# Layer 1's attention begun nine slots earlier, with short logits sharing a bank, biases loaded a group ahead, and GpSimd scaling by a column operand

## The chip, the cores and the metric

The kernel runs on one core of a Trainium2 chip. The metric is the time of one execution on the device, in microseconds (us). A core has a matrix engine (PE), three engines for elementwise work (DVE, the vector engine; ACT, the scalar engine; POOL, the GpSimd engine) and DMA queues, here driven by SP. Each engine takes its own instructions in order, and engines wait for each other through semaphores. PE writes into PSUM, which has eight banks of 512 float32 columns on 128 partitions; POOL cannot reach PSUM.

## The reference

Two layers on a sequence of 512 tokens of width 1024. Layer 0 mixes a stick-breaking attention with a short convolution, layer 1 is a sparse attention, and each is followed by a SwiGLU network. The change lies in layer 1's attention:

```python
def odd_mixer(h, w_in, q_gain, k_gain, w_out, rel_bias):
    proj = h @ w_in
    q, k, v, qi, ki, wi = jnp.split(proj, offsets([ATT_WIDTH, KV_WIDTH, KV_WIDTH, ...]), axis=-1)
    q = rms_norm(q.reshape(b, s, ATT_HEADS, HEAD_DIM), q_gain)     # 16 heads of 64
    k = rms_norm(k.reshape(b, s, KV_HEADS, HEAD_DIM), k_gain)      # 4 groups, 4 heads each
    ...
# dsa_attention, for each block of 128 queries:
        score = ...                                # indexer; the best 128 keys of each query are kept
        logits = (jnp.einsum('bqgrd,bqkgd->bqgrk', qb, k_sel) * HEAD_DIM ** -0.5 + bias)
        p = jax.nn.softmax(logits, axis=-1)
        return jnp.einsum('bqgrk,bqkgd->bqgrd', p, v_sel)
```

Instead of gathering keys, the kernel adds a mask of -1e30 to the logits of keys that were not chosen. Matrix operands are kept as a high and a low half (fp32r), so that a product is made of two or three matmuls.

## The kernel before

**Slots and events.** The projections are loops over weight tiles. After each three matmuls of 128x512 (`mm3`, or lines 232 to 234) they call `slot()`, which counts on and runs what `after(n, fn, key)` has put down for this slot, smaller keys first. So attention is woven into projections: its instructions stand, on every engine, at the places where the slots put them. In layer 1 this written order is kept for PE, DVE, ACT and POOL (`L1_ORDER`). When a projection is over, empty slots follow, in which nothing but attention stands.

**The projections of layer 1** come in this order: indexer, keys and values, queries of heads 0 to 7 (`ev_q0`), queries of heads 8 to 15 (`ev_q1`, the last query projection, 32 slots), then, after the empty slots, the output projection in two halves. At the end of the last query projection ACT copies each of its four results (`qn<-acc`) and squares it (`sq`, `sqx<-acc`, L966), DVE sums the squares (L967), and `head_norm` makes a reciprocal root of them on ACT (`hn_y`, L979), some small steps on DVE, and four products on POOL (L987). `turn_q` then transposes the queries (L999, tile `pt`) and `stack` writes their high half on ACT (L494) and the low half on POOL or DVE (L498); POOL works from a copy in SBUF (`qt`, L1045).

**Top-k.** DVE finds the kept keys by 16 rounds of MAX (L934) and MATCH_REPLACE (L937) on three query blocks, spread over the projections, and then writes the masks (L940). Query block 0 needs none.

**Attention** has 16 units, numbered n: group g = n // 4 (four heads) and query block qb = n % 4. A unit of query block qb has (qb + 1) x 128 keys, so logits are 128, 256, 384 or 512 wide. Unit n goes through these steps, at slots counted from its first, b:

- `logits` (b to b + 3, one head per slot): two matmuls (L507, L508) into one of two `z` banks, a third that adds the mask (L1084, not for qb = 0), and one DVE instruction that adds the bias and finds the maximum (L1085). For qb = 0 it also issues the DMA of the head's bias table, with four buffers (`rb`).
- `exps` (b + 4 to b + 7): DVE negates the four maxima (L1093); ACT makes exp and sum, one head per slot (L1095).
- `norms` (b + 8, b + 9): DVE takes the reciprocals `sm` (L1102); heads 0, 1 and 3 are scaled on POOL (L1105), head 2 on DVE (L1110).
- `turn_p` (b + 11 and on, one block of keys per slot): four transposes (L1118, tile `pt`), a high half on ACT (L1129), a low half on DVE (L1130).
- `prod` (b + 14 and on): six matmuls per block of keys into `po` (lines 105 to 107); then `keep` on ACT (L1150) and DVE (L1151).

Unit n begins at slot b = 4n + 32 - EARLY of the last query projection, with EARLY = 2.

Of the kernel before, what the change touches and what calls it, by code (L numbers as in the profile page):

```python
# [8 lines left out]
F32 = mybir.dt.float32  # L9
F32R = mybir.dt.float32r  # L10
ALU = mybir.AluOpType
# [4 lines left out]
P = 128  # L16
S = 512
# [14 lines left out]
LAG_K, T1P, B2, LAG_KLO, P1 = 2, 3, 'adbc', 2, 0  # L32
EARLY, SQ_ACT = 3, 256
DOT_PACE = 1
# [6 lines left out]
FILL = -3e38  # L41
# [1 line left out]
ARENA_KB = 104.5  # L43
X_SPANS = ((0, 1), (1, 2), (2, 4), (4, 6), (6, 8))

EARLY = 2
T1P = 4
LAG_K = 3
NORM_POOL = (0, 1, 3)
# [27 lines left out]
class Net:  # L77
# [762 lines left out]
    def layer1_mix(self):  # L840
        nc, I, tc = self.nc, self.I, self.tc
# [10 lines left out]
        qs, qsf = self.R(72.5, 16, S)  # L852
# [3 lines left out]
        with ExitStack() as es:  # L856
            sp = es.enter_context(tc.tile_pool(name="l1", bufs=2))
# [3 lines left out]
                    for qb in range(TB)]  # L861
            score = [None] + [wide[qb]()[:, 0] for qb in (1, 2)] + [self.ssq]
            mask = [None] + [sp.tile([P, (qb + 1) * P], F32R, name=f"mask{qb}", bufs=1)
                             for qb in (1, 2, 3)]
            eye = self.eye
# [77 lines left out]
            for qb, pace in zip((1, 2, 3), PACE):  # L943
                for r in range(16):
                    t = dots[qb] - self.slots + int(pace * r)
# [25 lines left out]
            def head_norm(hn, raw, dst, nh, pace):  # L971

                a, y, t = hn["a"], hn["y"], hn["t"]

                def chain():
                    nc.vector.tensor_tensor(a, a, r2.unsqueeze(2).to_broadcast([P, TB, nh]),
                                            op=ALU.mult)
                    nc.vector.tensor_scalar(a, a, EPS, None, op0=ALU.add)
                    nc.scalar.activation(y, a, AF.Abs_reciprocal_sqrt)  # L979

                def chain2():
                    self.newton(y, a, t)
                    nc.vector.tensor_tensor(y, y, self.rcol.unsqueeze(2).to_broadcast([P, TB, nh]),
                                            op=ALU.mult)

                def norm(tb):
                    nc.gpsimd.tensor_tensor(dst[tb], raw[tb],  # L987
                                            y[:, tb].unsqueeze(2).to_broadcast([P, nh, 64]),
                                            op=ALU.mult)
                self.after(2, chain, -1)  # L990
                self.after(LAG_CH, chain2, -1)
                for tb in range(TB):
                    self.after(LAG_CH + 1 + int(pace * tb), lambda tb=tb: norm(tb), 7)
                return LAG_CH + 1 + int(pace * 4)

            def turn(src, c, tag):
                pt = self.bank(tag, "pt")
                for tb in range(TB):
                    nc.tensor.transpose(pt[:, tb * P:(tb + 1) * P], src[tb][:, c * P:(c + 1) * P],  # L999
                                        self.ident)  # L1000
                return pt
# [17 lines left out]
            t = head_norm(hk, [t[:, :, 1] for t in d], [t[:, :, 0] for t in d], 4, 1)  # L1019
# [20 lines left out]
            def turn_q(qn, hf, c, tag):  # L1040
                pt = turn(qn, c, tag)

                if c in Q_POOL[hf]:
                    src, eng = self.wraw.tile([P, S], F32, name="qt", tag="raw"), nc.gpsimd
                    nc.scalar.copy(src, pt)  # L1045
                else:
                    src, eng = pt, nc.vector
                self.stack([(qs[:, h], qsf[:, h]) for h in (8 * hf + 2 * c, 8 * hf + 2 * c + 1)],
                            src, eng, LAG_LO)
# [10 lines left out]
            t = head_norm(h0, heads(q0[0]), heads(q0[0]), 8, 1.7)  # L1060
# [3 lines left out]
            order = [(qb, g) for g in range(4) for qb in range(TB)]  # L1064
            bias, us = {}, [{} for _ in order]

            def logits(n, r):
                (qb, g), u = order[n], us[n]
                nk = (qb + 1) * P
                t = slice(qb * P, nk)  # L1070
                h = 4 * g + r
                if r == 0:
                    u["mx"] = sp.tile([P, TB], F32, name="mx", bufs=3)
                    u["sm"] = sp.tile([P, TB], F32, name="sm", bufs=3)
                    u["ls"] = wide[qb]()
                if not qb:
                    bias[h] = sp.tile([P, S], F32, name="bias", tag="rb", bufs=4)
                    nc.sync.dma_start(bias[h], bass.AP(tensor=self.F.tensor,
                                                       offset=self.F.offset + h * 640,
                                                       ap=[[1, P], [1, S]]))  # L1080
                z = self.bank("z", "z")[:, 0:nk]
                self.qk(z, qs[:, h, t], kh[:, g, 0:nk], kl[:, g, 0:nk], not qb)
                if qb:
                    nc.tensor.matmul(z, eye, mask[qb], start=False, stop=True)  # L1084
                nc.vector.tensor_tensor_reduce(out=u["ls"][:, r], in0=z,  # L1085
                                               in1=bias[h][:, 0:nk][:, ::-1],
                                               scale=1.0, scalar=FILL, op0=ALU.add,
                                               op1=ALU.max, accum_out=u["mx"][:, r:r + 1])

            def exps(n, rs):  # L1090
                ls, mx, sm = us[n]["ls"], us[n]["mx"], us[n]["sm"]
                if rs[0] == 0:
                    nc.vector.tensor_scalar(mx, mx, -1.0, None, op0=ALU.mult)  # L1093
                for r in rs:
                    nc.scalar.activation(ls[:, r], ls[:, r], AF.Exp, bias=mx[:, r:r + 1],  # L1095
                                         accum_out=sm[:, r:r + 1])

            def norms(n, rs):
                ls, sm = us[n]["ls"], us[n]["sm"]
                nk = (order[n][0] + 1) * P  # L1100
                if rs[0] == 0:
                    nc.vector.reciprocal(sm, sm)  # L1102
                for r in rs:
                    if r in NORM_POOL:
                        nc.gpsimd.tensor_tensor(ls[:, r], ls[:, r],  # L1105
                                                sm[:, r:r + 1].to_broadcast([P, nk]), op=ALU.mult)
                    elif r in NORM_ACT:
                        nc.scalar.activation(ls[:, r], ls[:, r], AF.Copy, scale=sm[:, r:r + 1])
                    else:
                        nc.vector.tensor_scalar(ls[:, r], ls[:, r], sm[:, r:r + 1], None,  # L1110
                                                op0=ALU.mult)

            def turn_p(n, kb):
                u = us[n]
                self.turns += 1
                pt = self.bank("tbd"[self.turns % 3], "pt")
                for r in range(4):
                    nc.tensor.transpose(pt[:, r * P:(r + 1) * P],  # L1118
                                        u["ls"][:, r, kb * P:(kb + 1) * P], self.ident)
                i = self.turns % 4  # L1120
                if n >= 8 and i >= 2:

                    ph, pl = (sp.tile([P, S], F32R, name="pT", tag=f"n{2 * i - 4 + j}", bufs=1)
                              for j in range(2))
                    phf = ph.bitcast(F32)
                else:
                    o = (48.25, 52.25, 8, 12)[i]
                    (ph, phf), pl = self.R(o, S), self.R(o + 2, S)[0]
                nc.scalar.copy(ph, pt)  # L1129
                self.after(LAG_LO, lambda: nc.vector.tensor_tensor(pl, pt, phf, op=ALU.subtract), -1)  # L1130
                u[kb] = [p.rearrange("p (c e q) -> p c e q", c=2, e=2) for p in (ph, pl)]
# [13 lines left out]
            def keep(n):  # L1145
# [5 lines left out]
                self.after(LAG_K, lambda: nc.vector.tensor_tensor(  # L1151
                    al[:, c, t], po, ahf[:, c, t], op=ALU.subtract), -2)

            for n, (qb, g) in enumerate(order):
                b = 4 * n + 32 - EARLY
                for r in range(4):
                    self.after(b + r, lambda n=n, r=r: logits(n, r), 0)
                for r in range(4):
                    self.after(b + 4 + r // EXPS, lambda n=n, r=r: exps(n, (r,)), 0.5)
                    self.after(b + LAG_N + r // 2, lambda n=n, r=r: norms(n, (r,)), 3)  # L1160
                for kb in range(qb + 1):
                    self.after(b + LAG_C + kb, lambda n=n, kb=kb: turn_p(n, kb), 1)
                    self.after(b + LAG_C + LAG_P + kb, lambda n=n, kb=kb: prod(n, kb), 2)
                self.after(b + LAG_C + LAG_P + qb + 1, lambda n=n: keep(n), -1)
            start = self.slots + 32 - EARLY

# [10 lines left out]
            t = head_norm(h1, heads(q1), heads(q1), 8, 1)  # L1177
# [62 lines left out]
```

## Time and profile before

| | |
|---|---|
| median of 3 runs | 1212.41 us (1212.17 to 1212.91) |
| the profiled execution | 1214.13 us, of which its span 1212.4 us |
| PE busy | 1189.0 us, 98% of the span |
| PEld (weight loads) busy | 978.5 us |
| DVE, ACT, POOL busy | 652.9, 480.1, 143.8 us |
| the last query projection's end | about 700.3 us |
| attention without a projection | about 700 to 764 us |

Busy time is what the records of an engine cover. A matmul of 128x512 is recorded as 0.39 us, but the next one begins 0.23 us later, so PE counts as busy through short waits. Rows of the timeline give start, length, engine, line, operation, the tiles written and read, and in brackets how long the engine stood idle before and what ended it. An `x3` at the end merges neighbours into one row. `LDWEIGHTS` rows are left out here.

### The profile page before, as it was taken

The numbers are of one execution on the slowest core, as the hardware profiler recorded it, in microseconds if no ns is written. First come the engines' busy times: TensorE is split into PE (matmuls) and PEld (weight loads), VectorE is DVE, ScalarE is ACT, GpSimd is POOL, SyncE is SP. The second block draws the span as 40 slices with busy tenths as digits, with TensorE's granted clock in tenths as the row PEclk, the third lists the DMA queues.
The fourth block names the chain that finished last, engine by engine and source line by source line (L and its number), as shares of the span: only waits on it lengthen the run. The fifth ranks groups of instructions, "written<-read, shape, count | busy, mean of one in ns | idle before, by whom it ended". The sixth has DMA issues, their size and how long they took to land.

```text
span 1212.4 us, 14654 instructions
## 1 busy us (share of the span) xinstructions
PE 1189.0 (98%) x5547; PEld 978.5 (81%) x5547; DVE 652.9 (54%) x1067; ACT 480.1 (40%) x797; POOL 143.8 (12%) x217
## 2 busy tenths in 40 slices
PE   9999999999999999999999989999999999999998
PEld 7777878888888888888788868888888888888886
DVE  5679965655545443333379977745444343342222
ACT  5556634543434332222253577534332322322120
POOL 1234300200000000011001554312000000000000
PEclk9999999999999999999999999999999999999999
DMA  5322125878887632232346432223333333332430
GB/s 191 92 70 70 53 84 190 277 248 281 284 273 262 226 92 96 96 96 78 124 150 232 157 104 70 71 78 126 91 89 90 103 87 102 89 104 88 129 97 35
DMA packets 118583, 159.86 MB, mean 132 GB/s; under 512 B 6292, under 2 KB 91840, under 8 KB 118512
## 3 DMA queue, kind: packets, MB, share of 16 engines
q1 hardware_dynamic: 117712, 157.73, 40.1%
q10 hardware_dynamic: 800, 1.18, 0.3%
q8 instruction: 44, 0.72, 0.2%
q14 instruction: 27, 0.22, 0.1%
HBM read 131.00 MB, written 27.89 MB: 131 GB/s over the span
## 4 chain that ended last, share of the span: by engine, by line
PE 89%; DVE 6%; issue 2%; POOL 2%; ACT 0%; DMA 0%; POOLq 0%; DVEq 0%; ACTq 0%
PE acc L105 22%; PE acc L107 21%; PE acc L106 21%; PE acc L234 6%; PE acc L233 6%; PE acc L232 6%; PE pt L1118 1%; PE z L507 1%; PE z L508 1%; DVE om L532 1%; DVE wl L163 1%; PE po L106 1%; PE po L107 1%; DVE be L535 1%; PE po L105 1%
## 5 line engine op out<-in xcount | busy, mean ns | idle before, releaser
L105 PE MATMUL acc<-arena,wh 128*128 128x512 f32 (+2 forms) x1176 | 466.7, 397 | 1.9 <-DVE xT L728 1.0
L107 PE MATMUL acc<-arena,wl 128*128 128x512 f32 (+2 forms) x1176 | 458.2, 390 | 0.1
L106 PE MATMUL acc<-arena,wh 128*128 128x512 f32 (+2 forms) x1176 | 458.0, 389 | 0.0
L163 DVE TENSOR_TENSOR wl<-raw,wh 128x1024 fp32r<-128x1024 f32 (+1 forms) x167 | 202.9, 1215 | 285.3 <-ACT wh L162 285.0
L162 ACT CAST wh<-raw 128x1024 fp32r<-128x1024 f32 (+1 forms) x167 | 173.0, 1036 | 360.5 <-PE acc L106 155.7
L107 PEld LDWEIGHTS acc<-arena,wl 128*128 128x128 f32 (+1 forms) x1176 | 220.4, 187 | 49.9 <-DVE wl L163 0.4
L105 PEld LDWEIGHTS acc<-arena,wh 128*128 128x128 f32 (+1 forms) x1176 | 220.8, 188 | 46.9 <-DVE xT L728 2.1
L106 PEld LDWEIGHTS acc<-arena,wh 128*128 128x128 f32 (+1 forms) x1176 | 220.8, 188 | 43.6 <-issue 0.7
L232 PE MATMUL acc<-wh,arena 128*128 128x512 f32 x272 | 108.8, 400 | 0.0
L234 PE MATMUL acc<-wh,arena 128*128 128x512 f32 x272 | 108.4, 399 | 0.0
L233 PE MATMUL acc<-wl,arena 128*128 128x512 f32 x272 | 108.2, 398 | 0.0
L286 POOL TENSOR_TENSOR ssq<-ssq,sqx 128x512 f32<-128x512 f32 x12 | 18.2, 1520 | 371.7 <-ACT sqx L285 371.7
L234 PEld LDWEIGHTS acc<-wh,arena 128*128 128x128 f32 x272 | 51.5, 189 | 12.2
L815 DVE TENSOR_TENSOR pwl<-praw,pwh 128x1024 fp32r<-128x1024 f32 (+1 forms) x25 | 30.2, 1208 | 57.0 <-ACT pwh L814 57.0
L233 PEld LDWEIGHTS acc<-wl,arena 128*128 128x128 f32 x272 | 51.5, 189 | 11.6
L232 PEld LDWEIGHTS acc<-wh,arena 128*128 128x128 f32 x272 | 51.5, 189 | 11.5
L763 DVE TENSOR_TENSOR ft<-acc,rbc 128x512 f32<-128x512 f32 x44 | 30.0, 690 | 45.7 <-PE acc L107 45.6
L814 ACT CAST pwh<-praw 128x1024 fp32r<-128x1024 f32 (+1 forms) x25 | 25.9, 1036 | 68.5 <-DMA praw<-in_od_w_in_dram 38.2
L765 ACT ACTIVATE fs<-ft 128x512 f32<-128x512 f32 x44 | 27.6, 629 | 51.3 <-DVE ft L763 51.3
L507 PE MATMUL z<-arena 128*128 128x384 f32 (+3 forms) x120 | 40.7, 342 | 6.7 <-DVE mx L1085 4.1
L1085 DVE CUSTOM_DVE_ANT_0 L<-z,bias 128x128 f32<-128x128 f32 (+3 forms) x64 | 30.7, 485 | 22.2 <-PE z L1084 19.6
L770 DVE TENSOR_TENSOR fp<-acc,fs 128x512 f32<-128x512 f32 x44 | 30.4, 690 | 22.7 <-PE acc L107 22.7
(212 smaller groups left out, 1281.0 us busy)
## 6 DMA issues: line engine op xcount, KB each, us to landing
raw<-in_ffn_w_gate_dram SPq DMA_DIRECT2D x44, 512.0 KB, 3.7
raw<-in_ffn_w_up_dram SPq DMA_DIRECT2D x44, 512.0 KB, 3.8
raw<-in_ffn_w_down_dram SPq DMA_DIRECT2D x42, 512.0 KB, 3.7
l1h<-pwh SPq DMA_DIRECT2D x24, 512.0 KB, 2.7
l1l<-pwl SPq DMA_DIRECT2D x24, 512.0 KB, 3.1
wh<-l1h SPq DMA_DIRECT2D x24, 512.0 KB, 4.0
wl<-l1l SPq DMA_DIRECT2D x24, 512.0 KB, 4.5
raw<-in_ev_w_in_dram SPq DMA_DIRECT2D x23, 512.0 KB, 3.9
```

The lines of the kernel that those rows point to most:

```text
L105: mm(ps, wh, xh, start=first, stop=False)
L106: mm(ps, wh, xl, start=False, stop=False)
L107: mm(ps, wl, xh, start=False, stop=last)
L162: nc.scalar.copy(wh, raw)
L163: (lo or nc.vector).tensor_tensor(wl, raw, wh.bitcast(F32), op=ALU.subtract)
L232: mm(ps[tb], h[:, t], wh[:, k], start=c == 0, stop=False)
L233: mm(ps[tb], h[:, t], wl[:, k], start=False, stop=False)
L234: mm(ps[tb], l[:, t], wh[:, k], start=False, stop=c == kc - 1)
L507: self.nc.tensor.matmul(z, qs, kd, start=True, stop=False)
L770: nc.vector.tensor_tensor(p, ps, sil[m], op=ALU.mult)
L815: nc.vector.tensor_tensor(l, raw, h.bitcast(F32), op=ALU.subtract)
L1085: nc.vector.tensor_tensor_reduce(out=u["ls"][:, r], in0=z, in1=bias[h][:, 0:nk][:, ::-1], scale=1.0, scalar=FILL, op0=ALU.add, op1=ALU.max ...
```

## The change

It does six things, all in layer 1's attention (lines of the changed code are some 10 to 16 higher than before: L1085 becomes L1097, L1095 becomes L1107, L1105 becomes L1117, L1118 becomes L1130, L1173 becomes L1189).

1. EARLY goes from 2 to 11: unit n begins nine slots earlier in the program. Unit 0 now begins at slot 21 of 32 of the last query projection, and its first `turn_p` follows on that projection's last slot. The empty slots before the output projection become nine fewer. What the query projection's own events do (`turn_q`) stays at its slots.
2. Logits of query block 0 are made four heads in a slot into one `z` bank, of block 1 two heads per slot and bank; blocks 2 and 3 stay at one.
3. Biases are loaded by `load_bias`, 14 slots ahead of their group: two heads into one buffer of the pool that otherwise holds raw weights (`raw`, three buffers), two into `rb`.
4. The copies `qt` of the last queries use another buffer (`tmp`, one of it) instead of `raw`.
5. The count that picks banks and buffers in `turn_p` starts anew.
6. POOL scales by `tensor_scalar` with a column of 128x1 as the operand, instead of `tensor_tensor` with that column broadcast.

```diff
-EARLY = 2
+EARLY = 11
...
-                    src, eng = self.wraw.tile([P, S], F32, name="qt", tag="raw"), nc.gpsimd
+                    src = (sp.tile([P, S], F32, name="qt", tag="tmp", bufs=1) if hf else
+                           self.wraw.tile([P, S], F32, name="qt", tag="raw"))
+                    eng = nc.gpsimd
...
+            def load_bias(g):
+                pair = self.wraw.tile([P, 2, S], F32, name="bias2", tag="raw")
+                for r in range(4):
+                    h = 4 * g + r
+                    bias[h] = (pair[:, r] if r < 2 else
+                               sp.tile([P, S], F32, name="bias", tag="rb", bufs=4))
+                    nc.sync.dma_start(bias[h], ...)
...
-            def logits(n, r):
+            def logits(n, rs):
...
-                z = self.bank("z", "z")[:, 0:nk]
-                self.qk(z, qs[:, h, t], kh[:, g, 0:nk], kl[:, g, 0:nk], not qb)
...
+                bank = self.bank("z", "z")
+                zs = [bank[:, i * nk:(i + 1) * nk] for i in range(len(rs))]
+                for r, z in zip(rs, zs):
+                    h = 4 * g + r
+                    self.qk(z, qs[:, h, t], kh[:, g, 0:nk], kl[:, g, 0:nk], not qb)
+                    if qb:
+                        nc.tensor.matmul(z, eye, mask[qb], start=False, stop=True)
+                for r, z in zip(rs, zs):
+                    nc.vector.tensor_tensor_reduce(...)
...
-                        nc.gpsimd.tensor_tensor(ls[:, r], ls[:, r],
-                                                sm[:, r:r + 1].to_broadcast([P, nk]), op=ALU.mult)
+                        nc.gpsimd.tensor_scalar(ls[:, r], ls[:, r], sm[:, r:r + 1], None,
+                                                op0=ALU.mult)
...
+            self.turns = -1
+            for g in range(4):
+                self.after(max(1, 16 * g + 32 - EARLY - 14), lambda g=g: load_bias(g), -3)
             for n, (qb, g) in enumerate(order):
                 b = 4 * n + 32 - EARLY
-                for r in range(4):
-                    self.after(b + r, lambda n=n, r=r: logits(n, r), 0)
+                w = (4, 2, 1, 1)[qb]
+                for r in range(0, 4, w):
+                    self.after(b + r, lambda n=n, rs=tuple(range(r, r + w)): logits(n, rs), 0)
```

**PE, in the last query projection, just after the third transposition of the first queries.** L232 to L234 are one slot of the projection. Before:

```order
L999 MATMUL pt<-eye,qn 128x128 x4
L232 MATMUL acc<-wh,arena 128x512
L233 MATMUL acc<-wl,arena 128x512
L234 MATMUL acc<-wh,arena 128x512
L232 MATMUL acc<-wh,arena 128x512
L233 MATMUL acc<-wl,arena 128x512
L234 MATMUL acc<-wh,arena 128x512
L999 MATMUL pt<-eye,qn 128x128 x4
```

Now:

```order
L999 MATMUL pt<-eye,qn 128x128 x4
L232 MATMUL acc<-wh,arena 128x512
L233 MATMUL acc<-wl,arena 128x512
L234 MATMUL acc<-wh,arena 128x512
L507 MATMUL z<-arena 128x128
L508 MATMUL z<-arena 128x128
L507 MATMUL z<-arena 128x128
L508 MATMUL z<-arena 128x128
L507 MATMUL z<-arena 128x128
L508 MATMUL z<-arena 128x128
L507 MATMUL z<-arena 128x128
L508 MATMUL z<-arena 128x128
```

Unit 0's logits of all four heads stand now one slot after the third transposition and ahead of the fourth; each head's first matmul waits for POOL (the low half of that head's queries).

**ACT, at the end of the last query projection.** L1173 (now L1189) is the copy of a result, L966 its square, L1095 (now L1107) the exps of units 0, 1 and 2 by their widths, L979 the head norm's root. Before:

```order
L1173 COPY qn<-acc 128x512
L966 ACTIVATE sq<-acc 128x512
L979 ACTIVATE hn_y<-hn_a 128x32
L1095 ACT_TABLE_LOAD
L1095 ACTIVATE L,sm<-L,mx 128x128 x4
L1095 ACTIVATE L,sm<-L,mx 128x256 x4
L1129 CAST arena<-pt 128x512
L1095 ACTIVATE L,sm<-L,mx 128x384 x3
```

Now:

```order
L1107 ACTIVATE L,sm<-L,mx 128x256
L1189 COPY qn<-acc 128x512
L966 ACTIVATE sqx<-acc 128x512
L1107 ACTIVATE L,sm<-L,mx 128x256 x2
L1189 COPY qn<-acc 128x512
L966 ACTIVATE sq<-acc 128x512
L1107 ACTIVATE L,sm<-L,mx 128x256
L1141 CAST arena<-pt 128x512
L1107 ACTIVATE L,sm<-L,mx 128x384
L979 ACT_TABLE_LOAD
L979 ACTIVATE hn_y<-hn_a 128x32
L1107 ACT_TABLE_LOAD
```

The exps stand between the copies and squares, and the root now stands between unit 2's first and second exp, with a table load on each side of it (the first exps, some rows earlier, have one of their own as well).

**POOL, from the low halves of the first queries on.** L1105 (now L1117) scales, L987 is the head norm of the last queries, L498 a low half. Before:

```order
L498 TENSOR_TENSOR arena<-qt,arena 64x512 x8
L987 TENSOR_TENSOR qn<-qn,hn_y 128x512
L1105 TENSOR_TENSOR L<-L,sm 128x128 x2
L987 TENSOR_TENSOR qn<-qn,hn_y 128x512
L1105 TENSOR_TENSOR L<-L,sm 128x128
L987 TENSOR_TENSOR qn<-qn,hn_y 128x512 x2
L1105 TENSOR_TENSOR L<-L,sm 128x256 x3
L1105 TENSOR_TENSOR L<-L,sm 128x384 x3
L1105 TENSOR_TENSOR L<-L,sm 128x512 x3
```

Now:

```order
L498 TENSOR_TENSOR arena<-qt,arena 64x512 x8
L1117 TENSOR_SCALAR L<-L,sm 128x128 x3
L1117 TENSOR_SCALAR L<-L,sm 128x256 x3
L1117 TENSOR_SCALAR L<-L,sm 128x384 x2
L987 TENSOR_TENSOR qn<-qn,hn_y 128x512
L1117 TENSOR_SCALAR L<-L,sm 128x384
L987 TENSOR_TENSOR qn<-qn,hn_y 128x512 x3
L1117 TENSOR_SCALAR L<-L,sm 128x512 x3
```

The four head-norm products have moved from unit 0's scalings to units 2 and 3: one ahead of unit 2's last scaling and three ahead of unit 3's.

More of the change, by code (lines that the diff above doesn't have):

```diff
@@ L1065, in layer1_mix @@
             bias, us = {}, [{} for _ in order]
-            def logits(n, r):
+            def load_bias(g):
[4 more added lines that the diff above has]
+                               sp.tile([P, S], F32, name="bias", tag="rb", bufs=4))
+                    nc.sync.dma_start(bias[h], bass.AP(tensor=self.F.tensor,
+                                                       offset=self.F.offset + h * 640,
+                                                       ap=[[1, P], [1, S]]))
+            def logits(n, rs):
                 (qb, g), u = order[n], us[n]
@@ L1070, in logits @@
                 t = slice(qb * P, nk)
-                h = 4 * g + r
-                if r == 0:
+                if rs[0] == 0:
                     u["mx"] = sp.tile([P, TB], F32, name="mx", bufs=3)
@@ L1075, in logits @@
                     u["ls"] = wide[qb]()
[L1076 to L1080, printed above, removed]
-                z = self.bank("z", "z")[:, 0:nk]
-                self.qk(z, qs[:, h, t], kh[:, g, 0:nk], kl[:, g, 0:nk], not qb)
[L1083 to L1088, printed above, removed]
+                bank = self.bank("z", "z")
[6 more added lines that the diff above has]
+                for r, z in zip(rs, zs):
+                    nc.vector.tensor_tensor_reduce(out=u["ls"][:, r], in0=z,
+                                                   in1=bias[4 * g + r][:, 0:nk][:, ::-1],
+                                                   scale=1.0, scalar=FILL, op0=ALU.add,
+                                                   op1=ALU.max, accum_out=u["mx"][:, r:r + 1])
             def exps(n, rs):
```

## The prediction

> **What bounds the kernel now.** First the page's busy times, then the chip's stretches of 10 us through layer 1's attention, then who waited for whom on PE.
>
> ```profile
> span 1212.4 us, 14654 instructions
> PE 1189.0 (98%) x5547; PEld 978.5 (81%) x5547; DVE 652.9 (54%) x1067; ACT 480.1 (40%) x797; POOL 143.8 (12%) x217
> ...
> core 0: us, PE busy (x) PEld busy (x) DVE busy (x) ACT busy (x) POOL busy (x), PEclk, DMA share, GB/s
> 700.00:710.00 10.00, 6.95 (x37) 5.18 (x37) 6.97 (x36) 6.77 (x21) 4.10 (x6) 1.00 0.32 107
> 710.00:720.00 10.00, 8.60 (x57) 7.11 (x57) 8.16 (x28) 8.50 (x23) 5.39 (x8) 1.00 0.52 157
> 720.00:730.00 10.00, 8.89 (x69) 8.15 (x68) 8.69 (x25) 8.02 (x22) 4.92 (x6) 1.00 0.01 2
> 730.00:740.00 10.00, 8.37 (x57) 7.29 (x56) 7.07 (x21) 7.81 (x22) 6.23 (x8) 1.00 0.36 97
> 740.00:750.00 10.00, 9.06 (x58) 8.28 (x58) 7.54 (x28) 7.57 (x22) 5.45 (x6) 0.83 0.34 115
> 750.00:760.00 10.00, 9.66 (x71) 9.27 (x72) 7.61 (x25) 5.87 (x17) 2.17 (x6) 1.00 0.00 1
> ...
> PE z L507 <- DVE mx L1085: 4.1, 6, 1.1
> PE pt L1118 <- POOL L L1105: 3.3, 5, 1.3
> ...
> DVE L L1085 <- DMA bias<-F: 0.5, 1, 0.5
> ```
>
> PE is the bound, and the change removes no matmul, so it can only win back time in which PE stands or runs slowly. From 700 to 760 PE is idle for 3.05 + 1.40 + 1.11 + 1.63 + 0.94 + 0.34 = 8.5 us, and the granted clock of 0.83 in one stretch costs 10 x 0.17 = 1.7 us. A matmul that follows a pause costs about 0.15 us more than the pause (0.39 us recorded, 0.23 apart in a run), for some 20 pauses 3 us. So 13 us, 1.1% of the time, is all there is. But DVE and ACT are busy for 7 to 8.7 of 10 us here: PE's pauses come from the chain logits, maximum, exp, scaling, transposition, which runs through four engines in written order.
>
> **The early start.** In the last query projection unit 0's logits now follow one slot after the third transposition, at 691.70:
>
> ```profile
> 691.70 0.39 PE L232 MATMUL acc<-wh,arena 128*128 128x512 f32 x1
> 692.40 0.60 PE L999 MATMUL pt<-eye,qn 128*128 128x128 f32 x4
> ...
> 688.90 11.02 POOL L498 TENSOR_TENSOR arena<-qt,arena 64x512 fp32r<-64x512 f32 x8 [2.53 <-ACT arena L494]
> ...
> 693.05 0.68 DVE L934 MAX8 w<-ssq 128x8 f32<-128x512 f32 x1
> ```
>
> The first row is the slot that logits now precede, 0.70 us long by the second. POOL makes the low halves of heads 0 to 7 one after the other, 1.37 us each: those of heads 2 and 3 are there at 693.0 and 694.4. PE does heads 0 and 1 (0.35 us), then stands for 2.3 us in a stretch where it had no idle time. Nothing covers that. The new load_bias does not add to it: on SP its first pair stands ahead of the second weight tile of this projection, but its buffer is free by then.
>
> The maxima of unit 0 come after MAX (693.05) at 694.6 to 695.6 on DVE. From here exps and squares hold each other up: ACT's order is exp, copy, square, and DVE's is maximum, sum of squares, maximum.
>
> ```profile
> 695.84 0.59 ACT L1173 COPY qn<-acc 128x512 f32<-128x512 f32 x1 [0.72 <-PE acc L234]
> 696.32 0.60 ACT L966 ACTIVATE sqx<-acc 128x512 f32<-128x512 f32 x1
> 703.31 1.28 ACT L1095 ACT_TABLE_LOAD   x1
> 704.61 0.40 ACT L1095 ACTIVATE L<-L,mx 128x128 f32<-128x128 f32 x1
> 713.79 0.19 ACT L1095 ACTIVATION_READ_ACCUMULATOR L<-L,mx 128x1 f32 x1
> ...
> 701.61 0.69 DVE L967 TENSOR_REDUCE hn_a<-sq 128x8 f32<-128x512 f32 x1 [0.74 <-ACT sq L966]
> 703.21 0.42 DVE L1085 CUSTOM_DVE_ANT_0 L<-z,bias 128x256 f32<-128x256 f32 x1 [0.18 <-PE z L1084]
> ...
> 708.00 0.49 PE L1118 MATMUL pt<-eye,L 128*128 128x128 f32 x3
> 709.19 0.33 PE L1118 MATMUL pt<-eye,L 128*128 128x128 f32 x1 [0.70 <-POOL L L1105]
> ```
>
> With these lengths (copy and square 0.48 apart, exps 0.40 and 0.50, sums 0.6, maxima 0.2, 0.34 and 0.48 by width) I walk the new order. Unit 1's first logits leave PE at 698.5; its negated maxima come only behind unit 2's first maximum and the second sum, at 704.6; so the third square ends at 706.2, the third sum at 706.8, and unit 2's second maximum behind it at 707.3. It frees the bank that unit 2's last logits need, for which PE, done with the projection at about 706.0, waits 1.5 us. Unit 0's first transposition begins at about 708.05, against 708.00 now. So the nine slots of overlap are worth nothing by then but POOL's wait of 0.70 at 709.19.
>
> **Two more table loads.** The root of the head norm now stands among the exps, so ACT loads tables at 1.28 us twice more, between unit 2's first and second exp. By the walk unit 2's first exp runs at 710.1, the loads and the root take until 713.5, and its last exp ends at 715.7, against 713.98 now (the READ row's end): 1.7 us later.
>
> **POOL's scaling by a column.** No row shows this instruction. Its neighbours:
>
> ```profile
> L1105 POOL TENSOR_TENSOR L<-L,sm 128x512 f32<-128x512 f32 x12 | 12.7, 1087 | 11.2 <-DVE sm L1102 7.9 <-PE z L1084 3.3
> L1105 POOL TENSOR_TENSOR L<-L,sm 128x384 f32<-128x384 f32 x12 | 10.0, 860 | 10.4 <-DVE sm L1102 6.5 <-PE z L508 3.9
> L1105 POOL TENSOR_TENSOR L<-L,sm 128x128 f32<-128x128 f32 x12 | 4.6, 407 | 11.8 <-DVE sm L1102 11.7
> L652 POOL CAST arena<-kt 64x512 fp32r<-64x512 f32 x8 | 8.9, 1115 | 4.3 <-DVE kt L648 4.0
> L635 POOL MEMSET arena<- 64x512 f32 x6 | 3.1, 519 | 0.5 <-POOLq L1225 0.3
> L915 POOL TENSOR_SCALAR_AFFINE_SELECT L<-L 128x128 f32<-128x128 f32 x2 | 0.6, 296 | 35.1 <-DVE L L911 35.1
> L987 POOL TENSOR_TENSOR qn<-qn,hn_y 128x512 f32<-128x512 f32 x8 | 8.2, 1046 | 15.1 <-DVE hn_y L983 15.1
> ```
>
> From below it is bounded by a memset (519 of 1087, a factor of 0.48), which reads nothing; from above by a copy with one input (1115, 1.03). Nearest is the select with one input: 296 against 407 at 128 columns, 0.73. I take 0.72: 0.62 us at 384, 0.78 at 512. The Trainium skill ("GPSIMD Engine Reference", Elementwise — side-by-side cycle accounting) gives 1.03 to 1.8 cycles per element to bodies with one input against 2.6 for two; at 1.2 GHz that is 440 to 770 ns for 512 columns, an estimate from the page. By its lower end the factor would be about 0.4 and the forecast "faster", which is rival B; its 2.6 (1109 ns) agrees with the row's 1087, while the copy's 1115 does not agree with its one-input figure.
>
> On POOL one head-norm product (1.05) now precedes unit 2's last scaling and three precede unit 3's. Unit 2: reciprocal at 715.8, two scalings, a product and a scaling end at 718.7. Unit 3: three products to 721.8, three scalings to 724.15.
>
> ```profile
> 715.16 2.40 POOL L1105 TENSOR_TENSOR L<-L,sm 128x384 f32<-128x384 f32 x3 [2.00 <-DVE sm L1102]
> 721.23 3.04 POOL L1105 TENSOR_TENSOR L<-L,sm 128x512 f32<-128x512 f32 x3 [3.67 <-DVE sm L1102]
> 717.74 0.62 PE L1118 MATMUL pt<-eye,L 128*128 128x128 f32 x4
> 723.66 0.39 PE L507 MATMUL z<-arena 128*128 128x256 f32 x1 [0.97 <-DVE mx L1085]
> 724.12 0.92 PE L1118 MATMUL pt<-eye,L 128*128 128x128 f32 x4
> 740.05 0.33 PE L1118 MATMUL pt<-eye,L 128*128 128x128 f32 x1 [1.29 <-POOL L L1105]
> 732.06 0.33 PE L1118 MATMUL pt<-eye,L 128*128 128x128 f32 x1 [0.39 <-POOL L L1105]
> 727.15 1.27 ACT L494 CAST arena<-qt 64x512 fp32r<-64x512 f32 x2
> ```
>
> Unit 3's first transpositions now are done at about 724.7 (the row's end is a recorded tail later). They will be done at 724.3, but two transpositions of the last queries (2 x 0.44), which stand ahead of them today, then come later: as work goes, PE is 724.3 - (724.7 - 0.9) = 0.5 us behind. In between PE waits some 2 us for unit 1's high half (behind the table loads on ACT), 1.3 for unit 2 and 1.6 for unit 3.
>
> **From there to the output projection** the shift helps. The low halves on POOL no longer fall between the scalings of one short unit: the wait of 1.29 at 740.05 goes, with its 0.15, and the one of 0.39 at 732. With those the slow clock of 740 to 750 should go, which directly followed: 1.7. Together -3.6. Short logits sharing a bank and biases a group ahead save another 0.3 (DVE waited 0.5 once for a bias, and PE stood behind it). What comes new: `turn_q` for heads 12 and 13 now stands on ACT ahead of unit 7's last three exps (copy 0.6, two casts 1.27), and POOL's low half (2.6) ahead of unit 7's scalings. Walked, unit 7 is scaled 2.8 us after PE wants it, where it loses 1.3 now (of the 3.3 us that PE waits for scalings, 0.9 in two waits are left there, with 0.15 each for the matmul behind): +1.5. Such a pause can bring the slow clock back: half a chance of 1.7, +0.85. Of the clock the Trainium skill says ("TensorE: Matmul & The Clock Gate", Part 1) that it halves after about 3.4 us of idleness; by that alone a pause of 2.8 us would cost nothing, and the sum would be 0.85 lower. Here a pause of 1.29 us amid short matmuls was enough, so I keep the row's reading.
>
> Other queues: SP issues the same 16 biases, earlier, and raw weights for the next network behind them, whose use lies 70 us on. The new buffer for `qt` and the restarted count cost nothing that the walk shows.
>
> **The sum:** 0.5 - 3.6 - 0.3 + 1.5 + 0.85 = -1.05 us. It is made against the profiled execution (1214.13 us, of which 1212.4 are its span); the median of the runs is 1212.41, so 1211.4. No change, as far as a measurement tells, which is about 0.2%, 2.4 us.
>
> **The rivals.**
> A, the forecast: overlap given back through table loads and POOL, about 1211.4.
> B, faster: the scaling is cheap. On PE's path stand three scalings of 384 and six of 512, 3 x 0.86 + 6 x 1.09 = 9.1 us today; each tenth of the factor moves 0.9 us. At 0.48 that is -2.2; unit 7's wait then shrinks to a length that leaves the clock alone, -0.85: 1208.3. For it speaks that POOL ended the waits above, and that I may have walked the engines too strictly in step; against it, that below a factor of 0.55 PE's own work, not POOL, ends unit 3's wait.
> C, slower: the column operand is dearer than the tensor, as the copy with one input suggests. From a factor of 1.10 on (1.20 us at 512) the sum passes +2.4; at 1.5 it is 0.78 x 9.1 - 1.05 = +6.0, 1218.4. Against it: the select's 0.73.
> D, the early start does nothing or harm by itself: the 2.3 us of wait at heads 2 and 3 is certain; should the waits before unit 3 also bring two slow windows that I count as hidden behind POOL, +3.4 - 1.05: 1214.8.
>
> **How the numbers follow.** A 0.40, B 0.35, C 0.15, D 0.10, of which half ends within 0.2%, as its 2.35 us lies at that edge. Faster 0.35; within 0.2% 0.45; slower 0.20. The costs' ends give -1.05 - 2.2 - 0.85 = -4.1 and, with the copy's 1.03 (2.8) and a slow window more (1.7), +3.5; B and C reach beyond these, so I take 1207.0 to 1216.5, which leaves out about 0.1 on each side. A alone: 1209.5 to 1214.
>
> **What would show it.** A wait of PE for POOL L498 of about 2.3 us at 692, two more table loads near 711 and 712; first transposition of unit 0 near 708; PE waiting near 714 to 724 for ACT and POOL; scalings of 512 at 0.78 us; a pause at unit 7 near 745. I am wrong if POOL's scaling is below 0.6 or above 1.2 us, or if PE has no pauses around units 2 and 3.

## The result, and the profile after

The changed kernel takes 1229.21 us (median of four runs, 1228.0 to 1230.17), the kernel before 1212.29 (four runs): a ratio of 1.014, 95% interval 1.0126 to 1.0153. It is 16.9 us slower, where 1.05 us faster was forecast and 1216.5 was the range's upper end. The profiled execution took 1228.0 us with a span of 1226.3; before, 1214.13 and 1212.4. So 13.9 us lie between the two traces, and the same 13.9 already lie between them in the output projection (DVE's row of L728 at 821.96 before, at 835.83 now). The changed trace went into the attention 1.27 us ahead (the third transposition of the first queries is at 689.29, not 690.56), so the attention itself lost some 15.1 us. The lead looks like luck: from 50 to 60 us, in code that the change leaves alone, the clock was 0.83 before and 1.00 now, worth 10 x 0.17 = 1.7 us. A single trace carries that much luck. First the changed kernel's busy times, then its stretches of 10 us (columns as before), one row over the whole passage, and who waited for whom on PE from 685 to 835 us (total, times, longest):

```profile
span 1226.3 us, 14639 instructions
PE 1195.2 (97%) x5547; PEld 983.1 (80%) x5547; DVE 651.9 (53%) x1067; ACT 481.8 (39%) x799; POOL 160.5 (13%) x217
...
700.00:710.00 10.00, 8.10 (x38) 5.98 (x37) 7.95 (x27) 7.39 (x23) 2.09 (x4) 1.00 0.66 243
710.00:720.00 10.00, 6.78 (x36) 4.87 (x35) 6.62 (x28) 9.01 (x22) 6.91 (x7) 0.81 0.39 105
720.00:730.00 10.00, 7.96 (x41) 7.50 (x42) 4.36 (x15) 3.79 (x13) 8.04 (x7) 0.67 0.00 0
730.00:740.00 10.00, 10.00 (x68) 9.66 (x67) 6.59 (x19) 5.90 (x16) 1.77 (x3) 0.84 0.01 2
740.00:750.00 10.00, 7.56 (x51) 6.24 (x48) 8.44 (x30) 7.58 (x19) 5.42 (x6) 1.00 0.38 106
750.00:760.00 10.00, 8.22 (x42) 7.50 (x42) 4.51 (x15) 7.73 (x22) 8.17 (x6) 0.66 0.01 2
...
690.00:770.00 80.00, 66.75 (x387) 58.18 (x386) 51.71 (x175) 53.45 (x140) 45.79 (x43) 0.87 0.21 66
...
PE pt L1130 <- POOL L L1117: 8.2, 10, 1.5
PE z L507 <- DVE mx L1097: 2.5, 3, 1.2
PE po L105 <- DVE arena L1163: 2.0, 2, 1.2
PE po L105 <- ACT arena L1141: 1.6, 1, 1.6
PE z L507 <- POOL arena L498: 1.6, 2, 0.9
```

POOL is busy for 160.5 us where it was 143.8, and PE's wait for its scalings has grown from 3.3 to 8.2 us. Three waits are new: for the split of an older product (L1163), for ACT's high half (L1141) and for POOL's low halves of the queries (L498). The clock is below 1.00 in four of six stretches (0.50 throughout from 719 to 726 us); over the 80 us of the long row it costs 80 x 0.13 = 10.4 us, against 80 x 0.02 = 1.6 in the same row of before. PE's listed waits grew by 8.7 us (17.4 against 8.7, with small ones not shown here). Together that is more than was lost, as far as a pause inside a stretch at half the clock counts in both.

The scaling on POOL, from the groups of the changed kernel, with the shapes kept apart:

```profile
L1117 POOL TENSOR_SCALAR L<-L,sm 128x512 f32<-128x512 f32 x12 | 18.6, 1568 | 6.7 <-DVE sm L1114 6.7
L1117 POOL TENSOR_SCALAR L<-L,sm 128x384 f32<-128x384 f32 x12 | 15.4, 1298 | 13.2 <-DVE sm L1114 13.2
L1117 POOL TENSOR_SCALAR L<-L,sm 128x128 f32<-128x128 f32 x12 | 7.1, 609 | 12.6 <-DVE sm L1114 12.6
```

1568 against 1087 ns is a factor of 1.44, 1298 against 860 one of 1.51: the new scaling is dearer at every width. Where PE feels it is seen in rows chosen from PE, ACT, DVE and POOL:

```profile
691.68 0.33 PE L507 MATMUL z<-arena 128*128 128x128 f32 x1 [0.69 <-POOL arena L498]
693.02 0.33 PE L507 MATMUL z<-arena 128*128 128x128 f32 x1 [0.90 <-POOL arena L498]
707.39 0.60 PE L1130 MATMUL pt<-eye,L 128*128 128x128 f32 x4
715.81 0.38 PE L105 MATMUL po<-arena 128*128 128x256 f32 x1 [1.62 <-ACT arena L1141]
720.43 0.48 PE L1130 MATMUL pt<-eye,L 128*128 128x128 f32 x1 [1.54 <-POOL L L1117]
729.36 0.33 PE L1130 MATMUL pt<-eye,L 128*128 128x128 f32 x1 [1.10 <-POOL L L1117]
760.26 0.33 PE L1130 MATMUL pt<-eye,L 128*128 128x128 f32 x1 [1.11 <-POOL L L1117]
...
710.27 1.28 ACT L979 ACT_TABLE_LOAD   x1
711.82 1.28 ACT L1107 ACT_TABLE_LOAD   x1
...
723.62 0.42 DVE L1097 CUSTOM_DVE_ANT_0 L<-z,bias 128x256 f32<-128x256 f32 x1 [5.65 <-PE z L1095]
724.38 0.17 DVE L1114 RECIPROCAL sm<-sm 128x4 f32<-128x4 f32 x1
...
719.14 1.24 POOL L1117 TENSOR_SCALAR L<-L,sm 128x384 f32<-128x384 f32 x1
720.35 3.04 POOL L987 TENSOR_TENSOR qn<-qn,hn_y 128x512 f32<-128x512 f32 x3
724.66 4.65 POOL L1117 TENSOR_SCALAR L<-L,sm 128x512 f32<-128x512 f32 x3 [1.26 <-DVE sm L1114]
```

Unit 2 is scaled at 720.4 and unit 3 at 729.3; PE's transpositions stand right behind both. The first delay feeds the second: PE waits until 720.43 for unit 2, only then makes the logits of unit 5, and behind DVE's instruction on these (bias and maximum, 723.62; a "pass" below) stands the reciprocal of unit 3 (724.38), for which POOL waits 1.26 us.

### The profile page after: what moved, and what is told of

It is laid out like the page before. It is cut to its first block, busy times and chain, and to the rows that moved or that the text cites. A ratio compares the mean times of both kernels' runs of the same rounds, so it can differ in the third digit from the quotient of the medians.

```text
span 1226.3 us, 14639 instructions
## 1 busy us (share of the span) xinstructions
PE 1195.2 (97%) x5547; PEld 983.1 (80%) x5547; DVE 651.9 (53%) x1067; ACT 481.8 (39%) x799; POOL 160.5 (13%) x217
## 5 line engine op out<-in xcount | busy, mean ns | idle before, releaser
L232 PE MATMUL acc<-wh,arena 128*128 128x512 f32 x272 | 108.2, 398 | 0.0
L234 PE MATMUL acc<-wh,arena 128*128 128x512 f32 x272 | 107.8, 396 | 0.0
L286 POOL TENSOR_TENSOR ssq<-ssq,sqx 128x512 f32<-128x512 f32 x12 | 17.7, 1476 | 372.3 <-ACT sqx L285 372.3
L234 PEld LDWEIGHTS acc<-wh,arena 128*128 128x128 f32 x272 | 51.2, 188 | 12.2
L232 PEld LDWEIGHTS acc<-wh,arena 128*128 128x128 f32 x272 | 51.1, 188 | 11.2
L1117 POOL TENSOR_SCALAR L<-L,sm 128x128 f32<-128x128 f32 (+3 forms) x48 | 52.2, 1103 | 54.1 <-DVE sm L1114 47.7
L1097 DVE CUSTOM_DVE_ANT_0 L<-z,bias 128x128 f32<-128x128 f32 (+3 forms) x64 | 29.6, 487 | 38.0 <-PE z L1095 34.8
```

The costliest lines, as they stand in the source:

```text
L232: mm(ps[tb], h[:, t], wh[:, k], start=c == 0, stop=False)
L234: mm(ps[tb], l[:, t], wh[:, k], start=False, stop=c == kc - 1)
L1117: nc.gpsimd.tensor_scalar(ls[:, r], ls[:, r], sm[:, r:r + 1], None, op0=ALU.mult)
```

## The experiments

Three theories stood at first: 1, the column operand loses the time; 2, the early start does; 3, stretches at half the clock multiply whatever pause there is.

**One part undone, or one alone.** The first kernel takes the column operand back out:

```diff
-nc.gpsimd.tensor_scalar(ls[:, r], ls[:, r], sm[:, r:r + 1], None, op0=ALU.mult)
+nc.gpsimd.tensor_tensor(ls[:, r], ls[:, r], sm[:, r:r + 1].to_broadcast([P, nk]), op=ALU.mult)
```

> The changed kernel with one part undone: GpSimd scales the halves with tensor_tensor and the broadcast norm again; the early start, the shared bank and the biases ahead stay. Theory 1 (the column operand loses the time: its passes take 1.44 to 1.50 times the old ones, 1568 against 1087 ns at 512 columns, and TensorE waits for them in the last pass): nearly all of the 16.9 us come back, 1209 to 1214 us, and the wait of pt for L falls from 8.2 to under 4 us. Theory 2 (the early start loses it: the pauses of TensorE at heads 2 and 3 of the first unit and the two more table loads of ScalarE): little comes back, 1223 to 1229 us, with the pauses at 691.7 and 715.8 still there. Theory 3 (pauses of either kind set off stretches at half the clock, six in the changed kernel, 1.7 us lost in each): the time follows the count of such stretches, each one left being worth 1.7 us.

Measured 1216.98 us, ratio to before 1.0038 (1.0026 to 1.0051). 12.2 us come back, not all: the time lies between the ranges of theories 1 and 2. Between the two traces (1228.0 and 1219.37 us) the waits for the scalings fall from 8.2 to 4.0, and the clock from 690 to 770 rises from 0.87 to 0.96, up to 7.2 us. The second kernel has the `+` and `-` of that diff swapped, on the kernel before:

> The kernel before with one part of the change alone: GpSimd scales the halves by a column operand with tensor_scalar. Theory 1 (the column operand loses the time): 1222 to 1230 us, with L's passes at about 0.6, 0.94, 1.3 and 1.57 us for 128, 256, 384 and 512 columns. Theory 2 (the early start loses it): 1212 to 1216 us, since the late units have the slack for the longer passes. By the prediction's own pricing of a dearer column operand, at 1.47 times the old pass: 1212.3 + 9.1 x (1.47 - 1.10) + 2.4 = 1218 us. Theory 3 (half-clock stretches): above 1218 only if the granted clock between 700 and 830 us shows three or more stretches at a half where the kernel before has one.

Measured 1222.9, ratio 1.0083 (1.007 to 1.0097): 10.6 us by the column operand alone. PE's waits for scalings, from 690 to 835 us:

```profile
PE pt L1118 <- POOL L L1105: 10.8, 11, 2.3
```

Before they were 3.3 in five: the late units do not have the slack that theory 2 gave them. The other two kernels have `EARLY = 2`, one with the column operand, one without:

```diff
-EARLY = 11
+EARLY = 2
```

> The changed kernel with the attention's early start undone (two spare slots at its head as before instead of eleven); the column operand, the shared bank and the biases ahead stay. Theory 1 (the column operand loses the time): 1222 to 1230 us, as with the column operand alone. Theory 2 (the early start loses it): 1211 to 1215 us. If both lose something that adds: about midway, 1217 to 1222.

Measured 1232.78, ratio 1.0164 (1.0149 to 1.018): slower than with the early start.

> The changed kernel with both the early start and the column operand undone: only the shared bank of short logits and the biases a group ahead are left. Theory 1 and theory 2 alike: these parts are worth nothing much, 1211 to 1213 us (the prediction had them at -0.3 us). A rival: the shared bank makes a unit's second logits wait for the first's readers, and the time comes out at 1214 or more.

Measured 1218.5, ratio 1.0047 (1.0034 to 1.0059). So the early start gains, 3.6 us with the column operand and 1.5 without, and theory 2 falls. And the rest, shared banks and biases ahead, loses 6.2 us. Only the rival in that expectation had such a time, though not by its mechanism: PE waits 2.2 us for a `z` bank here, 4.1 before. New are waits for the split of an older product (L1163, 2.4 us) and for DVE's scaling (1.6); the one for DVE's low half (L1142) has grown from 0.3 to 2.2. Theory 3 cannot be tried alone, since no kernel here sets the clock.

**Which part of the rest.** From that last kernel the sharing is taken out (first lines of the diff); then the sharing alone is put into the kernel before; then the sharing is taken out of the kernel with the early start and the tensor operand; then the count of transposition banks alone is restarted in the kernel before (last line):

```diff
-                w = (4, 2, 1, 1)[qb]
+                w = 1
...
+            self.turns = -1
```

> The kernel with the late start and tensor_tensor (1218.5 us), and one logits tile a bank again, four slots a unit; left of the change are the biases a group ahead, the buffer of qt and the restarted count of transposition banks. Theory S (sharing costs the 6 us: it puts the four maxima of a short unit in one slot, so DVE gives the split of an older product and the low halves late, and the three slots behind hold no logits for TensorE): 1211 to 1213.5 us, and the waits of po for L1163 (2.4 us) and of the pt for DVE's L (1.6 us) are gone. Theory B (the biases in the ring of raw weights and the restarted count cost them): 1217 to 1219 us.

Measured 1212.82, ratio 1.0004 (0.9994 to 1.0013): the 6 us are gone, and with them the waits for L1163 and for DVE's scaling.

> The kernel before with only the shared bank of short logits (four logits of 128 columns in one slot, or two pairs of 256). Theory S: 1216 to 1219.5 us, with the waits of po for the split two units back. Theory B: 1211 to 1213.5 us.

Measured 1227.99, ratio 1.0128 (1.0114 to 1.0142), more than expected, 15.1 us. Here the biases are still loaded in the slot that reads them, now four at once. DVE's and PE's waits from 685 to 835 us name it:

```profile
DVE L L1090 <- DMA bias<-F: 6.4, 7, 1.9
...
PE po L105 <- DVE arena L1156: 7.0, 2, 4.0
PE po L106 <- DVE arena L1135: 4.0, 3, 3.7
```

So loading the biases a group ahead is worth nothing by itself (1212.82 against 1212.91 before) but saves 9.5 us of what the sharing costs (1227.99 less 1218.5).

> The early start and the biases ahead, with tensor_tensor on GpSimd and one logits tile a bank: the parts that the runs so far don't speak against. From the sums of single parts (the early start gained 1218.5 - 1217.0 = 1.5 us with tensor_tensor; theory S gives 6.2 back): 1210.8 us, so about 1209 to 1212.5 and a little below the kernel before. Theory B: 1216 to 1218. Theory 2 of before (the early start by itself loses where the sharing doesn't cover it, 2.3 us of pause at heads 2 and 3): 1213 to 1216.

Measured 1211.47, ratio 0.9987 (0.9978 to 0.9996): the early start without sharing and without the column operand beats both kernels, by 1.4 us of before and 17.7 of the changed one.

> The kernel before with only the count of transposition banks restarted, so that banks and the buffers of the transposed probabilities are one place on in their rotation. Theory S: no change, 1211.5 to 1213.5 us. Theory B in its second form (the rotation makes a transposition wait for a bank that is read late): 1214 to 1218 us.

Measured 1212.78, ratio 1.0005 (0.9996 to 1.0014): nothing.

**Inside the two losses.** On the kernel of 1211.47 us, `w = (4, 1, 1, 1)[qb]` and `w = (1, 2, 1, 1)[qb]`; on the kernel before, `tensor_scalar` by a constant, which leaves out the norm; and, on the kernel of 1211.47 us again, `EARLY = 7`:

> The early start with tensor_tensor and unshared logits (1211.5 us), with only the four logits of 128 columns put in one bank and one slot again. All sharing costs 1217.0 - 1211.5 = 5.5 us there. Theory S1 (DVE's first pass over a shared bank starts only when the last matmul into that bank is through, and the reciprocal, the split of the older product and the low half stand behind four passes): the fours carry most of it, 1214 to 1217 us, with a wait of po for DVE's L1163 of about 1.2 us at two of the four-key units. Theory S2 (the pairs of 256 columns, whose three slots without logits leave TensorE nothing to do, carry it): 1211 to 1213 us.

Measured 1217.48, ratio 1.0037 (1.0023 to 1.0051).

> The same with only the pairs of 256-column logits sharing a bank. Theory S1: 1211 to 1213.5 us. Theory S2: 1214 to 1217 us, with waits of pt for DVE's scaling (L1122) of 0.7 and 0.95 us as in the kernel that shares all.

Measured 1212.54, ratio 1.0001 (0.9992 to 1.001). The fours carry it, 6.0 us against 1.1 (5.5 with both: the two do not simply add). Rows chosen from PE and DVE at unit 4, first with the fours shared, then without (two kernels, two fences):

```profile
741.00 0.33 PE L507 MATMUL z<-arena 128*128 128x128 f32 x1 [0.63 <-DVE mx L1097]
741.84 0.28 PE L508 MATMUL z<-arena 128*128 128x128 f32 x1
743.80 0.35 PE L105 MATMUL po<-arena 128*128 128x256 f32 x1 [0.79 <-DVE arena L1163]
...
742.25 0.29 DVE L1097 CUSTOM_DVE_ANT_0 L<-z,bias 128x128 f32<-128x128 f32 x1 [0.69 <-issue]
742.89 0.28 DVE L1097 CUSTOM_DVE_ANT_0 L<-z,bias 128x128 f32<-128x128 f32 x1
743.17 0.17 DVE L1114 RECIPROCAL sm<-sm 128x4 f32<-128x4 f32 x1
743.26 0.39 DVE L1163 TENSOR_TENSOR arena<-po,arena 128x256 fp32r<-128x256 f32 x1
```

```profile
738.18 0.33 PE L507 MATMUL z<-arena 128*128 128x128 f32 x1 [0.63 <-DVE mx L1097]
739.75 0.33 PE L105 MATMUL po<-arena 128*128 128x256 f32 x1
...
738.75 0.29 DVE L1097 CUSTOM_DVE_ANT_0 L<-z,bias 128x128 f32<-128x128 f32 x1
739.04 0.17 DVE L1114 RECIPROCAL sm<-sm 128x4 f32<-128x4 f32 x1
739.13 0.40 DVE L1163 TENSOR_TENSOR arena<-po,arena 128x256 fp32r<-128x256 f32 x1
```

Unshared, the first pass starts 0.57 us after its logits, and one pass precedes the reciprocal and the split (L1163), which starts 0.95 after the first logits. Shared, the first pass starts 1.25 after, behind the bank's last matmul (741.84), and four passes stand ahead (the first and the last are shown): the split starts 2.26 after. PE's next product waits for it.

> The kernel before, whose GpSimd scales by the constant 0.5 with tensor_scalar: the rows that GpSimd scales are left without their norm, and GpSimd doesn't wait for the reciprocal. It is the duration that matters. If tensor_scalar itself is dear on GpSimd: 1.5 to 1.6 us at 512 columns, as with the column. If the column operand makes it dear: 0.5 to 0.8 us at 512, the one-input pass that the prediction assumed.

One run, 1210.2 us. The group of 512 columns:

```profile
L1105 POOL TENSOR_SCALAR L<-L 128x512 f32<-128x512 f32 x12 | 17.8, 1504 | 1.5 <-ACT L L1095 1.5
```

1504 ns with a constant, 1568 with the column: it is `tensor_scalar` on POOL that is dear, and the column adds 64 ns. The time is short all the same: POOL here waits for the exp alone, not for the reciprocal, and PE's waits from 685 to 835 us have none for a scaling.

> The early start without sharing and with tensor_tensor, begun 4 slots later (seven spare slots in place of eleven). If the pauses at heads 2 and 3 of the first unit (1.6 us for GpSimd's low halves) are a net loss that a later begin avoids: 1209 to 1210.5 us. If what is won at the front is given back behind it at ScalarE's exps, the begin doesn't matter: 1211 to 1212. If the later begin only loses overlap: 1212 to 1213, towards the late start's 1212.8.

Measured 1213.82, ratio 1.0007 (0.9998 to 1.0015), 2.4 us worse than eleven slots and above all three ranges. That the pauses are a net loss falls. By the ratio nothing of the early start's gain is left (the late start has 1.0004); why not even a part of it is left is not shown.

**What in the fours costs.** Three variants of the kernel of 1217.48 us: the bank kept, with each logits and its pass in a slot of their own; all in one slot, with a bank each; and the passes spread alone (the diff is this one's):

```diff
+                for i, (r, z) in enumerate(zip(rs, zs)):
+                    if i:
+                        self.after(i, lambda r=r, z=z: maxima(r, z), 0)
+                    else:
+                        maxima(r, z)
```

> From the early start with tensor_tensor and unshared logits (1211.5 us): the four logits of 128 columns share a bank, but each stands in its own slot with its pass behind it. If the bank itself costs (a wait for the bank's last matmul): 1214 to 1217.5 us. If the bunching in one slot costs, of matmuls or of passes: 1210.5 to 1212.5 us.

Measured 1214.74, ratio 1.0016 (1.0007 to 1.0025), in the range of a bank that costs. It is no clean test of the bank: a new wait came in. PE's waits from 685 to 835 us:

```profile
PE z L507 <- DVE mx L1099: 8.3, 11, 2.2
```

(2.7 in six unshared.) With the bank shared over four slots, each write into it waits for the pass over its earlier part.

> The same start, the four logits of 128 columns in one slot, each in a bank of its own (two in the ring). If the bank costs: 1211 to 1213 us. If the bunching costs, of matmuls or of passes: 1215 to 1219 us, with TensorE waiting besides for the pass that frees a bank.

Measured 1218.4, ratio 1.0044 (1.003 to 1.0058). In the range of a bunching that costs, but no clean test either: with two banks in the ring PE waits 6.0 us in nine for one, again against 2.7 in six.

> The same start, the four logits in one bank and one slot, but the passes of DVE one a slot, as when unshared. If the four passes in a row ahead of the reciprocal, the split and the low half cost: 1210.5 to 1212.5 us, perhaps a little under the unshared kernel. If the matmuls' bunching (TensorE without logits for three slots) costs: 1214.5 to 1217.5 us. If the first pass's wait for the bank's last matmul costs: 1213 to 1215 us, since that wait stays and the rest goes.

Measured 1215.43, ratio 1.0021 (1.0012 to 1.0031). Spreading the passes gives back 2.0 of the 6.0 us. Of the other 4.0, the pauses of 0.7 and 0.9 us at heads 2 and 3 of unit 0 are in both kernels with the four logits in one slot and a shared bank, and not in the unshared one, whose heads 2 and 3 stand two and three slots on, at 693.60 and 694.60. How the remaining 2.4 divide between the first pass's wait and the slots left without logits stays open. Nor need the pauses cost their full length: with the late start sharing costs 5.7 us (1218.5 less 1212.82) without any wait for POOL's low halves.

## Why the prediction was wrong

**The failed step that weighs most is the scaling factor.** It was taken as 0.72 from the select's 296 against 407 ns, with 1.03 as its upper end; measured are 1.44 to 1.51. The nearest row was one instruction of another kind at one width, and it had not been asked what it does with its operand. The prediction's own sign came true, a scaling above 1.2 us (1.57). It is `tensor_scalar` on POOL that is dear, not the column (1504 ns with a constant). Rival C named a dearer scaling, at a chance of 0.15, and gave 1218.4 at a factor of 1.5, 7.0 over the forecast; the runs make it 12.2, and no rival reached the measured time. C counted the longer scalings on PE's path alone. It lacked the way from unit 2's delay to unit 3's, seen above, and the clock: with the column operand taken out the clock gives back up to 80 x 0.09 = 7.2 us in the trace, some of it lying over pauses. The two are not separated by a run.

**The second is "short logits sharing a bank and biases a group ahead save another 0.3".** Sharing costs 5.5 us by the medians of two sets of runs (1216.98 against 1211.47), 6.2 by their ratios to the kernel before (1.0038 against 0.9987). The step counted DVE's one wait for a bias and banks for PE, but not what four passes in a row delay behind them on DVE: the reciprocal, the split and the low half, for which PE waits (in the changed kernel 0.79 us for the split, at 747.60). The walk of the engines had these orders; it had been made closely only up to unit 3. The pause at heads 2 and 3 came (0.69 and 0.90 as recorded, not 2.3, though POOL's low halves came when they were forecast), yet it belongs to the sharing, not to the early start that it was booked to: unshared, there is none.

**The clock.** Half a chance of one more slow stretch was booked, 0.85 us, and one stretch less, 1.7; in the trace the clock cost 8.8 us more than before. Waits of 0.5 to 1.6 us between short matmuls came with it, none longer. But the prediction's reading that a pause of 1.29 us "was enough" does not hold: where only the count is restarted the same pause (1.27 us at 738.86) was followed by a clock of 1.00 from 740 to 750, and the pauses of 0.69 and 0.90 at heads 2 and 3 stood in a clock of 1.00 in the changed kernel and of 0.83 without its column operand (690 to 700). More pauses went with a lower clock over the whole passage (0.87 with 17.4 us of waits, 0.98 with 8.7); what sets off a single stretch is not shown. By the Trainium skill ("TensorE: Matmul & The Clock Gate", Part 1) the clock halves after some 3.4 us of idleness, which does not cover this trace, whose longest wait from 690 to 770 us is 1.62. The same part of the Trainium skill also tells, without a threshold, of a kernel in which frequent short idles made the clock go back and forth, and with that this trace agrees.

**What held.** The trace's times are to be read with the 1.27 us by which it was ahead. The two table loads came at 710.27 and 711.82 (forecast "near 711 and 712"); unit 0's first transposition at 707.39 (708.05); unit 2's last exp ended at 715.3 (715.7): with the lead added, right to within 1 us or so. Units 2 and 3 were scaled at 720.4 and 729.3 instead of 718.7 and 724.15: three scalings of 512 took 4.65 us, not 2.34, the products ahead of them were done at 723.4, not 721.8, and the reciprocal kept POOL waiting for 1.26 us more. At unit 7 PE stood for 1.1 us at 760.26, not 2.8; PE itself came late, which may be why. The restarted count costs nothing, as said. And the early start's worth, "+0.5" up to unit 3 and the waits saved behind it: by itself it gains 1.4 us (1211.47 against 1212.82 with the late start), near the forecast in size, though the two intervals just touch. That overlap is given back through table loads fits the trace without sharing, where PE waits 1.25 us for ACT's high half behind them (714.46); no run shows that this alone limits the gain.

By the ratios, which take out how the kernel before differs between sets of runs, the terms are 12.4 us for the column operand (1.014 less 1.0038), 6.2 for the sharing and -1.6 for the rest. They add up to the whole loss by construction, each being a step from one kernel to the next; the parts are not independent. The column operand costs 10.6 us on the kernel before and 14.3 with the late start and the sharing (1232.78 less 1218.5), and the sharing 15.1 where the biases are not loaded ahead.

## What to carry to other kernels

Before an instruction is exchanged on an engine, its price is wanted at the width in use; where no row has that form, the range must reach well beyond the nearest rows, and a chance of 0.15 for the dear side was too little. Instructions merged into one slot for the sake of one engine are to be followed on the queue of the next one: what stands behind them there is what gets late. And where TensorE works in short pieces between pauses, a term that makes pauses should be priced with a slower clock as a risk: here it came with up to 7.2 us beside 4.2 us of shorter waits.

## What was not expected of the hardware

`tensor_scalar` on GpSimd takes 609 ns at 128 columns and 1568 at 512, 2.50 ns a column, where `tensor_tensor` with a broadcast column takes 407 and 1087, 1.77 a column, though it reads a second operand. With a constant it takes 1504 at 512. And a stretch at half the clock needs no long idleness: over 80 us in which PE was busy for 66.75 and waited 1.62 at most, the clock was 0.87 on average. Nor does it come each time: the same code from 50 to 60 us had 0.83 in one trace and 1.00 in another.
